# The second weight block of the FFN input matrix: its sum S2 made during the mixing stage, S1 and S3 made later

## The chip, the cores and the metric

The kernel runs on one core of a Trainium2 chip. The metric is the device time of one execution in microseconds (us). PE is the matrix engine (TensorE), DVE the vector engine (VectorE), ACT the scalar engine (ScalarE), POOL is GpSimd, and SP the engine that only issues transfers here. Every engine works off its own queue of instructions in order.

## The reference, cut to what matters

One layer of a streaming encoder, one sequence of 1024 rows with 1024 channels, all in float32. A mixing sub-layer ends with an output projection, `x = x + g1 * (merged @ w_o)`. The feed-forward sub-layer (FFN) follows:

```
h2 = rms_norm(x, norm_ffn_g) * (1 + sc2) + sh2
a, bgate = split(h2 @ w_ffn_in)              # w_ffn_in: 1024 x 5632
x = x + g2 * ((silu(a) * bgate) @ w_ffn_out) # then a last rms_norm
```

The change concerns the product `h2 @ w_ffn_in`, and the stage with `w_o` before it.

## The kernel before, in words

**Arithmetic on PE.** A float32 operand is split into a high and a low part. `split_w` (L214) does it for a weight tile of 128 x 1024: ACT writes the high part `wh` with a cast (L220), DVE the low part `wl` with a subtraction (L221). There are three buffers for `wh` and three for `wl`, so the split of a product's weights has to wait until the product three places before is done. Each block of a product then takes three matmuls (`mm3`, L340): `wh` with the high activations (L348), `wh` with the low ones (L349), `wl` with the high ones (L351). One product is 24 matmuls of 128 x 512.

**Seven products instead of eight.** A "dual" is a weight block of two by two tiles 11, 12, 21, 22, which is multiplied with two by two blocks of activations by a Strassen-Winograd scheme in seven products, run in the order `PRODUCTS = "1265734"`. Products 1, 2 and 4 use the tiles 11, 12 and 22 as they are. The others use sums of tiles: product 5 uses S1 = 21 + 22, product 7 uses S3 = 21 + 11, product 6 uses S2 = 11 + S1, and product 3 uses 12 + S2. `dual_units` (L227) returns for each product a function that loads what is missing, adds and splits. The adds run on DVE: S1 at L240, S3 at L242, S2 at L244, 12 + S2 at L261. With `early == 2` product 6 loads 21, 22 and 11 and makes all three sums, each in place (S1 in the buffer of 22, S3 in that of 21, S2 in that of 11), and products 5 and 7 only split.

**Loads.** `load` (L204) takes the next buffer of 4 KB per partition for a raw tile and issues the transfer on SP. The buffers rotate over two pools (`rawp` with three, `rawbp` with two); a third pool, `raw_a` with one, joins at the start of the FFN (L1231). SP waits for the buffer that a transfer needs, with all later transfers behind it. `next_w` and `fetch` make the units of a list `plan` two products ahead.

**Order of the stages here.** `mix(i, h)` (L1020) makes one block of the projection with `w_o`, for the half `h` of the rows: 24 matmuls, a DVE instruction that adds the residual (L1028), a transfer out, a square on ACT (L1030) and a running sum on DVE (L1036). With `h == 1` and `i == 0` it is followed by `norm_2_first` (L1053): all of the normalised activations of the first half of the rows. The last five `w_o` tiles of the second half are split again while this runs. Then the FFN starts. The first products are ordered by `in_order` (L1104), as (dual, product): (0,1) (0,2) (1,1) (1,2) (2,1), then 6 5 7 3 4 of dual 0, then 6 5 7 3 4 of dual 1, then dual 2 and so on, eleven duals. Between them DVE and ACT make the activations that the products need: `norm_2_half` (L1062; the tiles x, t2 with their parts t2h and t2l) and `norm_2_sums` (L1073; t5, t7, t3, t4 with high and low parts, split at L388 and L389, and the subtractions for t4 at L393).

**Orders written out by hand.** `tc.issue_after(ins)` queues an instruction behind another one of its engine. `in_unit` (L1107) queues the adds and splits of (0,7), (0,3), (0,4) and (1,6) behind the splits of the activations traced before. `in_evac` (L1134) reads the results out of the accumulators: for dual 0 it queues the add of product 3 (L1150) behind `dual_units.ins`, the last S2 that was traced, and what follows behind the split traced last. All else is ordered by a scheduler, by the order in which the program text gives the instructions and by when they could run.

**Memory.** The pool `diff` has one buffer of 1054 elements per partition, used by the depthwise convolution (`conv`, L823), long before. It and the pool `uc` are closed at the fifth product after the first five (L1230), and what is opened then lies over them: by the allocation, the buffer of `raw_a` and the second of the two `x1a` buffers overlap that of `diff`.

Of the kernel before, what the change touches and what calls it, by code (L numbers as in the profile page):

```python
# [35 lines left out]
F32 = mybir.dt.float32  # L36
F32R = mybir.dt.float32r
AF = mybir.ActivationFunctionType
ALU = mybir.AluOpType

P = 128
D = 1024
T = 1024
# [3 lines left out]
FC = DFF // P  # L47
SK = 3
CK = 31
# [32 lines left out]


AHEAD = 2

# [19 lines left out]
PRODUCTS = "1265734"  # L107
# [14 lines left out]
def block_kernel(ctx: ExitStack, tc: tile.TileContext, x0, xT, c, vecs, ada, w_first, w_plain, w_duals,  # L122
                 w_short, w_conf, w_o, w_fi, w_fo, w_last, outT):
    nc = tc.nc
# [4 lines left out]
    def open_pool(name, bufs, stack=None, **kw):  # L129

        p = tc.tile_pool(name=name, bufs=bufs, reuse_waits="tile", **kw)
        return p, (stack.enter_context(p) if stack else p.__enter__())
# [16 lines left out]
    ucp, diffp = (p for _, p in phase_1)  # L149
# [17 lines left out]
    def f32(t):  # L167
        return t.bitcast(F32)
# [28 lines left out]
    raws = [rawp] * 3 + [rawbp] * 2  # L197

    def raw_tile(n=1024):

        raws.append(raws.pop(0))
        return raws[-1].tile([P, 1024], F32, tag="raw", name="raw")[:, :n]

    def load(src, n=1024):  # L204
        raw = raw_tile(n)
        nc.sync.dma_start(raw, src)
        return raw

    pool_los = []
# [4 lines left out]
    def split_w(raw, n, after=(), lo_engine=nc.vector):  # L214
        wh = whp.tile([P, 1024], F32R, tag="wh", name="wh")[:, :n]
        wl = wlp.tile([P, 1024], F32R, tag="wl", name="wl")[:, :n]
        with ExitStack() as order:
            for ins in after:
                order.enter_context(tc.issue_after(ins))
            hi = nc.scalar.copy(wh, raw)  # L220
            lo = lo_engine.tensor_tensor(wl, raw, f32(wh), ALU.subtract)  # L221
        split_w.hi, split_w.lo = hi.ins, lo.ins
        if n == T and lo_engine is nc.gpsimd:
            pool_los.append((hi.ins, lo.ins))
        return wh, wl

    def dual_units(mats, n, early=0, eng=nc.vector):  # L227


        a = {}  # L230

        def get(*blocks):
            for b in blocks:
                a[b] = load(mats[("11", "12", "21", "22").index(b)], n)

        def sums(which):

            if "1" in which:
                a["s1"] = a["22"] if early == 2 else raw_tile(n)
                eng.tensor_tensor(a["s1"], a["21"], a["22"], ALU.add)  # L240
            if "3" in which:
                eng.tensor_tensor(a["21"], a["21"], a["11"], ALU.add)  # L242
            if "2" in which:
                dual_units.ins = eng.tensor_tensor(a["11"], a["11"], a["s1"], ALU.add).ins  # L244

        def unit(m):
            if early == 2:
                get(*{"1": ("11",), "2": ("12",), "6": ("21", "22", "11"), "3": ("12",), "4": ("22",)}.get(m, ()))
            elif early:
                get(*{"1": ("11",), "2": ("12", "21", "22", "11")}.get(m, ()))  # L250
            elif m == "1":
                get("11", "12", "21", "22")
            if m in "12":
                w = split_w(a["1" + m], n, (), eng)
                if eng is nc.gpsimd:
                    sums("13" if m == "1" else "2")
                return w
            if m == "6" and eng is not nc.gpsimd:
                sums("132")
            if m == "3":  # L260
                eng.tensor_tensor(a["12"], a["12"], a["11"], ALU.add)  # L261
            return split_w(a[{"6": "11", "5": "s1", "7": "21", "3": "12", "4": "22"}[m]], n, (), eng)

        return {m: (lambda m=m: unit(m)) for m in PRODUCTS}

    def apart_units(mats, eng):

# [40 lines left out]

    def next_w(ahead=AHEAD):

        fetch(ahead + 1)
        return ready.pop(0)
# [71 lines left out]
    def t_pair(name):  # L384
        return hl_tile(name + "h"), hl_tile(name + "l")

    def t_split(src, hi, lo):
        t_split.act = nc.scalar.copy(hi, src).ins  # L388
        t_split.ins = nc.vector.tensor_tensor(lo, src, f32(hi), ALU.subtract).ins  # L389
# [12 lines left out]
    def rstd_end(ss, eps, r, t, exp):  # L402

        nc.vector.scalar_tensor_tensor(out=t, in0=r, scalar=-0.5, in1=r, op0=ALU.mult, op1=ALU.mult)
        nc.vector.scalar_tensor_tensor(out=t, in0=ss, scalar=eps, in1=t, op0=ALU.add, op1=ALU.mult)
        nc.vector.scalar_tensor_tensor(out=r, in0=t, scalar=1.5, in1=r, op0=ALU.add, op1=ALU.mult)
        return r
# [38 lines left out]
    def first_w(k):  # L446

        w = next_w(min(AHEAD, KC - 1 - k))
        if k >= KC - KEPT:
# [48 lines left out]
    def norm_start(acc, name, n=H, tile_of=g_tile, ss_tile=ps_tile):  # L498
        ss = ss_tile("ss")
        acc = acc if isinstance(acc, list) else [acc]  # L500
        for t in acc:
            norm_start.ins = nc.tensor.matmul(ss[:, :n], ones, t, start=t is acc[0], stop=t is acc[-1]).ins
        return rstd_start(ss, eps1, name, n, tile_of)
# [106 lines left out]
    def again_w(i):  # L610

        if i < KEPT:
            fetch(i // 2)
            return kept.pop(0)
        return next_w(1 if i < KC - 2 else AHEAD)

# [305 lines left out]
    def load_b(i):  # L922

        loaded.append((i, load(ada[i])))
        if len(loaded) > 1:
            with tc.issue_after(split.ins):
                modulation_of(*loaded.pop(0))
# [110 lines left out]
    def h2_of(k, h, r2, hi_lo=None):  # L1038

        t = x1[k][:, halves[h]]  # L1040
        nc.vector.scalar_tensor_tensor(out=t, in0=t, scalar=aff2[:, k : k + 1], in1=r2, op0=ALU.mult, op1=ALU.mult)
        if hi_lo:
            hi, lo = hi_lo
            nc.scalar.activation(hi, t, AF.Identity, bias=modc(24 + k))
            nc.vector.scalar_tensor_tensor(
                out=lo, in0=t, scalar=modc(24 + k), in1=f32(hi), op0=ALU.add, op1=ALU.subtract
            )
        nc.scalar.activation(t, t, AF.Identity, bias=modc(24 + k))
        return t
# [3 lines left out]
    def norm_2_first():  # L1053

        r2 = rstd_end(*norm_start(sums[0], "r2"))
        for k in range(KC):
            ts["12"[k // KH]][k % KH] = hl = t_pair(f"h2{k}")
            h2_of(k, 0, r2, hl)
# [14 lines left out]
    def norm_2_sums(m):  # L1073
# [3 lines left out]
        with tc.issue_after(t_split.ins), tc.issue_after(t_split.act):  # L1077
# [5 lines left out]
            for k in range(KH):  # L1083
                ts[m][k] = t_pair("t" + m)
                t_split({"5": x1[k][:, halves[0]], "7": b12[k], "3": b22[k], "4": b21[k]}[m], *ts[m][k])

    sums = {}
    for h in range(2):
        for i in range(KC):
            mix(i, h)  # L1090
            if h == 0:
                load_b(32 + i)
            if (h, i) == (0, KC - 1):
                modulation_of(*loaded.pop())
            if h == 1 and i == 0:
                for k in range(KC):
                    affine(aff2, k, 32, vec, V_GFFN)
                norm_2_first()


    N_IN = FC // 2
    EARLY = [2, 2, 1] + [0] * (N_IN - 3)
    in_units = [dual_units([w_fi[d, m] for m in range(4)], 1024, EARLY[d]) for d in range(N_IN)]
    in_order = [(0, "1"), (0, "2"), (1, "1"), (1, "2"), (2, "1")] + [(d, m) for d in range(2) for m in PRODUCTS[2:]]  # L1104
    in_order += [(d, m) for d in range(2, N_IN) for m in PRODUCTS if (d, m) != (2, "1")]

# [7 lines left out]
    ha = {}  # L1114
    in_banks = [{} for _ in range(N_IN)]

# [84 lines left out]
    def group_load(g, m):  # L1201
        to[g, m] = [t_load((g * GROUP + i, m)) for i in range(GROUP)]

    def in_product(d, m, between=None):
        late = EARLY[d] == 1
        if late and m == "2":
            for p in range(2):
                in_evac(d)(p, "1", in_banks[d]["x", p])
        product(in_banks[d], m, ts[m], None if late and m == "1" else in_evac(d), between,
                z_tile=ps2_tile if d in (0, 2) else ps_tile)  # L1210
        if d == N_IN - 1:
            group_load(0, m)
# [13 lines left out]
    for i, (d, m) in enumerate(in_order[5:]):  # L1226
        if i < 4:
            norm_2_sums("5734"[i])
        elif i == 4:
            close(*phase_1)  # L1230
            raws.append(open_pool("raw_a", 1, side="right", stack=ctx)[1])  # L1231
            x1ap = open_pool("x1a", 2, side="right", stack=ctx)[1]
            phase_2 = [open_pool("gi", 7), open_pool("stage", 3, side="right")]
            gip, stagep = (p for _, p in phase_2)
        with ExitStack() as order:
            if d < 2:
                order.enter_context(tc.issue_after(mm3.ins))
            in_product(d, m)
        if m == PRODUCTS[-1]:
            if 2 <= d < 6:  # L1240
                with tc.issue_after(in_evac.ins):
                    for b in range(40 + 2 * (d - 2), 42 + 2 * (d - 2)):
                        modulation(b, x1ap.tile([P, T], F32, tag="x1", name="ada"))
            hid_set(d)
# [24 lines left out]
    n = 2 * GROUP * P  # L1269
# [20 lines left out]
    for f in range(REST, FC, 2):  # L1290
        for oh in range(2):
            raw = load(w_last[(f - REST) // 2, oh])
# [161 lines left out]
```

## Time and profile before

| | |
|---|---|
| median of three runs | 1476.24 us (1476.24 to 1478.43) |
| the profiled execution, its own time | 1477.93 us |
| its span, first to last instruction | 1476.2 us |
| PE busy | 1462.0 us, 99% |
| DVE busy | 1177.7 us, 80% |
| ACT busy | 617.0 us, 42% |
| POOL busy | 513.3 us, 35% |
| moved by transfers | 245.36 MB, mean 166 GB/s |

All times within the run are us from the start of the span. A row of a timeline gives start, duration, engine, line, operation and tiles, and in brackets how long the engine had been idle before and what released it; a duration of a matmul reaches over the start of the next one, so the distance of two starts is what a matmul costs. A row by stages gives for each engine its busy time and the number of instructions, then the clock granted to PE and the share of the transfer engines.

### The profile page before, as it was taken

Reading aid. Unit: us, or ns where it says so; the run is one execution under the profiler, and the core shown is the slowest. Engines: PE = TensorE matmul, PEld = TensorE weight load, DVE = VectorE, ACT = ScalarE, POOL = GpSimd, SP = SyncE. Lnnn points to the kernel's source line nnn. Section 1 sums busy time; section 2 is a strip of 40 time slices with the busy share of each in tenths; the row PEclk is TensorE's granted clock in tenths of the full one; section 3 lists DMA queues with packets and bytes.
Section 4 is the critical chain, followed back from the end, with each engine's and each line's share of the span. In section 5 each row is a group of like instructions: output and inputs, shape, how many; then the busy total and the mean of one; then the engine's idle time right before and its main releaser. Section 6 shows DMA issues by size and latency. Waiting matters only on the chain.

```text
span 1476.2 us, 17809 instructions
## 1 busy us (share of the span) xinstructions
PE 1462.0 (99%) x6475; PEld 1200.4 (81%) x6475; DVE 1177.7 (80%) x1623; ACT 617.0 (42%) x896; POOL 513.3 (35%) x459
## 2 busy tenths in 40 slices
PE   9999999999999999999999999999999999999997
PEld 5888888888888888878888878888888888888887
DVE  7999888887998969999687699777777765677755
ACT  4653433333333335555235465444444443222235
POOL 0036677767877771111022001101111015535005
PEclk9999999999999999999999999999999999999999
DMA  8522213222222267376685337655455449988403
GB/s 342 188 64 72 100 58 128 72 86 100 91 67 86 82 219 285 105 237 213 200 311 172 117 100 235 209 176 168 150 192 166 146 149 371 357 287 276 156 1 115
DMA packets 83274, 245.36 MB, mean 166 GB/s; under 512 B 9585, under 2 KB 11761, under 8 KB 83186
## 3 DMA queue, kind: packets, MB, share of 16 engines
q1 hardware_dynamic: 42352, 136.01, 27.6%
q0 software_dynamic: 36944, 95.44, 19.6%
q10 hardware_dynamic: 3890, 12.78, 2.3%
q8 instruction: 51, 0.84, 0.2%
q14 instruction: 37, 0.30, 0.1%
HBM read 181.79 MB, written 62.39 MB: 165 GB/s over the span
## 4 chain that ended last, share of the span: by engine, by line
PE 91%; DVE 6%; DMA 1%; issue 1%; ACT 1%; POOL 0%; POOLq 0%; DVEq 0%; ACTq 0%
PE bank L351 11%; PE bank L348 11%; PE bank L349 11%; PE x L351 7%; PE x L348 7%; PE x L349 7%; PE z L349 4%; PE z L348 4%; PE z L351 4%; PE y L349 3%; PE y L348 3%; PE y L351 3%; PE yb L351 2%; PE yb L348 2%; PE yb L349 2%; PE mix L349 2%
## 5 line engine op out<-in xcount | busy, mean ns | idle before, releaser
L220 ACT CAST wh<-raw 128x1024 fp32r<-128x1024 f32 (+2 forms) x254 | 256.3, 1011 | 485.2 <-PE bank L349 133.6
L221 POOL TENSOR_TENSOR wl<-raw,wh 128x1024 fp32r<-128x1024 f32 x84 | 204.5, 2444 | 81.8 <-ACT wh L220 81.8
L221 DVE TENSOR_TENSOR wl<-raw,wh 128x1024 fp32r<-128x1024 f32 (+2 forms) x170 | 195.0, 1147 | 47.5 <-ACT wh L220 46.2
L838 DVE SCALAR_TENSOR_TENSOR c<-diff,vec,c 128x512 f32<-128x512 f32 x232 | 171.0, 753 | 4.4
L1170 POOL DMA_DIRECT2D hid<-stage x71 | 37.8, 533 | 347.0 <-DVE stage L389 341.0
L348 PE MATMUL bank<-th,wh 128*128 128x512 f32 x288 | 112.0, 389 | 0.0
L349 PE MATMUL bank<-tl,wh 128*128 128x512 f32 x288 | 112.0, 389 | 0.0
L351 PE MATMUL bank<-th,wl 128*128 128x512 f32 x288 | 112.0, 389 | 0.0
L838 DVE SCALAR_TENSOR_TENSOR c<-u,wsum,c 128x512 f32<-128x512 f32 x112 | 84.3, 753 | 2.6
L240 POOL TENSOR_TENSOR raw<-raw 128x1024 f32<-128x1024 f32 x12 | 29.2, 2430 | 130.4 <-DVE wl L221 92.8
L388 ACT CAST stage<-g 128x512 fp32r<-128x512 f32 x62 | 38.4, 622 | 65.9 <-DMA hid<-stage 35.4
L351 PEld LDWEIGHTS bank<-th,wl 128*128 128x128 f32 x288 | 54.1, 188 | 11.3
L349 PEld LDWEIGHTS bank<-tl,wh 128*128 128x128 f32 x288 | 54.1, 188 | 11.2
L348 PEld LDWEIGHTS bank<-th,wh 128*128 128x128 f32 x288 | 54.1, 188 | 11.2
L389 DVE TENSOR_TENSOR stage<-g,stage 128x512 fp32r<-128x512 f32 x62 | 42.4, 689 | 25.3 <-ACT stage L388 25.3
L1196 POOL DMA_DIRECT2D th<-hid x71 | 38.0, 535 | 53.2 <-PE x L351 31.9
L348 PE MATMUL x<-th,wh 128*128 128x512 f32 x144 | 56.1, 390 | 0.0
L349 PE MATMUL x<-tl,wh 128*128 128x512 f32 x144 | 56.0, 389 | 0.0
L351 PE MATMUL x<-th,wl 128*128 128x512 f32 x144 | 56.0, 389 | 0.0
L348 PE MATMUL yb<-zsh,wh 128*128 128x512 f32 x128 | 49.8, 389 | 0.0
L349 PE MATMUL yb<-zsl,wh 128*128 128x512 f32 x128 | 49.8, 389 | 0.0
L351 PE MATMUL yb<-zsh,wl 128*128 128x512 f32 x128 | 49.8, 389 | 0.0
(798 smaller groups left out, 4211.3 us busy)
## 6 DMA issues: line engine op xcount, KB each, us to landing
hid<-stage POOLq DMA_DIRECT2D x71, 512.0 KB, 4.4
raw<-in_w_fi SPq DMA_DIRECT2D x51, 512.0 KB, 3.7
raw<-in_w_duals SPq DMA_DIRECT2D x48, 512.0 KB, 3.5
th<-hid POOLq DMA_DIRECT2D x71, 256.0 KB, 5.7
tl<-hid POOLq DMA_DIRECT2D x71, 256.0 KB, 5.7
ada<-in_ada SPq DMA_DIRECT2D x24, 512.0 KB, 5.9
raw<-in_ada SPq DMA_DIRECT2D x24, 512.0 KB, 4.6
raw<-in_w_fo SPq DMA_DIRECT2D x24, 384.0 KB, 5.7
```

Of the source, the lines that this page charges most:

```text
L220: hi = nc.scalar.copy(wh, raw)
L221: lo = lo_engine.tensor_tensor(wl, raw, f32(wh), ALU.subtract)
L240: eng.tensor_tensor(a["s1"], a["21"], a["22"], ALU.add)
L348: nc.tensor.matmul(ps, wh, xh, start=first, stop=False, skip_group_check=again)
L349: nc.tensor.matmul(ps, wh, xl, start=False, stop=False, skip_group_check=again)
L351: mm3.ins = nc.tensor.matmul(ps, wl, xh, start=False, stop=last, skip_group_check=again).ins
L388: t_split.act = nc.scalar.copy(hi, src).ins
L389: t_split.ins = nc.vector.tensor_tensor(lo, src, f32(hi), ALU.subtract).ins
L838: tap.ins = nc.vector.scalar_tensor_tensor(out=out, in0=src[:, s : s + H], scalar=wt, in1=acc, op0=ALU.mult, op1=ALU.add).ins
L1170: nc.gpsimd.dma_start(hid_dram[key], s)
L1196: nc.gpsimd.dma_start(t, hid_dram[key][:, s])
```

## The change

For dual 1 alone, the generator `begin` makes S2 ahead of time, in three steps behind the blocks 2, 3 and 4 of the second half of `mix` (`S2_AT`). Step one loads 21 and 22. Step two adds S1 in the buffer of 22 and loads 11. Step three adds S2 = 11 + S1 into the buffer of `diff`. Each load is queued behind the last load traced before it. Product 6 of dual 1 then only splits S2; product 5 loads 21 and 22 once more and makes S1, product 7 loads 11 once more and makes S3, product 3 adds S2 to 12 as before. `raw_a` is still opened at the same place, but joins the rotation four products later. The rest of the diff moves the making of `in_units` ahead of the `mix` loop.

```diff
+S2_AT = (2, 3, 4)
...
     def load(src, n=1024):
         raw = raw_tile(n)
-        nc.sync.dma_start(raw, src)
+        load.ins = nc.sync.dma_start(raw, src).ins
         return raw
...
+        def begin():
+            with tc.issue_after(load.ins):
+                get("21", "22")
+            yield
+            eng.tensor_tensor(a["22"], a["21"], a["22"], ALU.add)
+            with tc.issue_after(load.ins):
+                get("11")
+            yield
+            a["s2"] = diffp.tile([P, T + CK - 1], F32, tag="diff", name="s2")[:, :n]
+            eng.tensor_tensor(a["s2"], a["11"], a["22"], ALU.add)
+            yield
+
+        def unit_begun(m):
+            get(*{"1": ("11",), "2": ("12",), "5": ("21", "22"), "7": ("11",), "3": ("12",), "4": ("22",)}.get(m, ()))
+            if m == "5":
+                sums("1")
+            elif m == "7":
+                sums("3")
+            elif m == "3":
+                eng.tensor_tensor(a["12"], a["12"], a["s2"], ALU.add)
+            return split_w(a[{"1": "11", "2": "12", "6": "s2", "5": "s1", "7": "21", "3": "12", "4": "22"}[m]], n, (), eng)
+
         def unit(m):
+            if "s2" in a:
+                return unit_begun(m)
...
+            if h == 1 and i in S2_AT:
+                next(in_units[1]["begin"])
...
-            raws.append(open_pool("raw_a", 1, side="right", stack=ctx)[1])
+            raw_a = open_pool("raw_a", 1, side="right", stack=ctx)[1]
...
+        elif i == 8:
+            raws.append(raw_a)
```

More of the change, by code (lines that the diff above doesn't have):

```diff
@@ L262, in unit @@
             return split_w(a[{"6": "11", "5": "s1", "7": "21", "3": "12", "4": "22"}[m]], n, (), eng)
-        return {m: (lambda m=m: unit(m)) for m in PRODUCTS}
+        return {m: (lambda m=m: unit(m)) for m in PRODUCTS} | {"begin": begin()}
     def apart_units(mats, eng):
@@ L1085, in norm_2_sums @@
                 t_split({"5": x1[k][:, halves[0]], "7": b12[k], "3": b22[k], "4": b21[k]}[m], *ts[m][k])
+    N_IN = FC // 2
+    EARLY = [2, 2, 1] + [0] * (N_IN - 3)
+    in_units = [dual_units([w_fi[d, m] for m in range(4)], 1024, EARLY[d]) for d in range(N_IN)]
     sums = {}
@@ L1098, in block_kernel @@
                 norm_2_first()
-    N_IN = FC // 2
-    EARLY = [2, 2, 1] + [0] * (N_IN - 3)
-    in_units = [dual_units([w_fi[d, m] for m in range(4)], 1024, EARLY[d]) for d in range(N_IN)]
+            if h == 1 and i in S2_AT:
+                next(in_units[1]["begin"])
     in_order = [(0, "1"), (0, "2"), (1, "1"), (1, "2"), (2, "1")] + [(d, m) for d in range(2) for m in PRODUCTS[2:]]
```

## The prediction

> **What bounds the kernel now.** I read the page first, then the waits of PE, then the timelines of PE, DVE and ACT around the place that they name.
>
> ```profile
> PE 1462.0 (99%) x6475; PEld 1200.4 (81%) x6475; DVE 1177.7 (80%) x1623; ACT 617.0 (42%) x896; POOL 513.3 (35%) x459
> PE 91%; DVE 6%; DMA 1%; issue 1%; ACT 1%; POOL 0%; POOLq 0%; DVEq 0%; ACTq 0%
> ```
>
> PE is busy for 1462.0 of 1476.2 us, so the number of matmuls sets the time, and this change alters none of them. An edit can only win where PE stands still. The second line is the chain that ended last: 6% of it lies on DVE, so somewhere DVE sets the pace.
>
> ```profile
> PE lead L344 <- ACT x L432: 2.3, 1, 2.3
> PE x L348 <- ACT wh L220: 1.2, 1, 1.2
> PE clock L535 <- DVE eps L183: 1.1, 1, 1.1
> PE bank L348 <- ACT wh L220: 0.6, 2, 0.4
> ```
>
> These are all of PE's listed waits (total, times, longest). The first and third are in the opening, the fourth in the products with the short convolution. The second, 1.2 us for a cast of weights, is in the FFN. The timeline of PE shows it:
>
> ```profile
> 876.16 0.62 PE L348 MATMUL x<-t4h,wh 128*128 128x512 f32 x2
> ...
> 881.37 0.39 PE L351 MATMUL x<-t4h,wl 128*128 128x512 f32 x1
> 882.98 0.50 PE L348 MATMUL x<-t2h,wh 128*128 128x512 f32 x1 [1.22 <-ACT wh L220]
> ...
> 888.92 0.39 PE L348 MATMUL z<-t5h,wh 128*128 128x512 f32 x1
> ...
> 894.36 0.39 PE L348 MATMUL x<-t7h,wh 128*128 128x512 f32 x1
> ```
>
> t4 is product (0,4), t2 here product (1,6), then come (1,5) and (1,7). From 888.92 to 894.36 one undisturbed product takes 5.44 us, 0.227 for each of 24 matmuls. The last matmul of (0,4) starts at 881.37, so (1,6) could start at 881.60 and (1,5) 5.44 later, at 887.04. It starts at 888.92. The stall at the head of (1,6), with the waits for `wl` in its first matmuls, costs 888.92 - 887.04 = 1.9 us. What DVE and ACT do meanwhile:
>
> ```profile
> 875.62 2.50 DVE L389 TENSOR_TENSOR t4l<-x,t4h 128x512 fp32r<-128x512 f32 x4
> 878.03 1.22 DVE L240 TENSOR_TENSOR raw<-raw 128x1024 f32<-128x1024 f32 x1
> 879.29 1.23 DVE L242 TENSOR_TENSOR raw<-raw 128x1024 f32<-128x1024 f32 x1
> 880.55 1.22 DVE L244 TENSOR_TENSOR raw<-raw 128x1024 f32<-128x1024 f32 x1
> 881.69 1.28 DVE L1150 TENSOR_TENSOR g<-z,g 128x512 f32<-128x512 f32 x2
> 882.96 1.22 DVE L221 TENSOR_TENSOR wl<-raw,wh 128x1024 fp32r<-128x1024 f32 x1
> ```
> ```profile
> 873.94 2.43 ACT L388 CAST t4h<-x 128x512 fp32r<-128x512 f32 x4
> 881.88 2.00 ACT L220 CAST wh<-raw 128x1024 fp32r<-128x1024 f32 x2 [5.52 <-DVE raw L244]
> ```
>
> DVE works without a pause: the low parts of t4, then S1, S3 and S2 of dual 1, and only after S2 can ACT cast the weights of (1,6). ACT has been idle for 5.52 us before that cast. So the stall is the three adds, 1.2 us each, in front of the cast.
>
> ```profile
> 786.00:826.00 40.00, 40.00 (x176) 32.75 (x175) 29.73 (x39) 22.29 (x32) 7.57 (x14) 1.00 0.58 184
> 826.00:859.00 33.00, 32.87 (x143) 26.22 (x142) 28.95 (x40) 18.12 (x29) 0.54 (x1) 1.00 0.24 72
> 859.00:882.00 23.00, 22.76 (x101) 18.52 (x99) 22.78 (x32) 14.57 (x24) 0.00 (x0) 1.00 0.44 137
> 882.00:900.00 18.00, 16.96 (x73) 13.73 (x74) 16.31 (x22) 11.62 (x18) 3.72 (x7) 1.00 0.68 221
> 900.00:1200.00 300.00, 300.00 (x1325) 248.40 (x1324) 222.16 (x278) 132.43 (x194) 31.91 (x60) 1.00 0.54 176
> ```
>
> By stages (after the length: busy PE, weight load, DVE, ACT, POOL; then PE clock): DVE fills 22.78 of the 23 us ahead of the stall, but 29.73 of 40 in the second half of mix, where the adds go. From 900 to 1200 PE does not pause. The second row lacks 0.13 us of PE, which I leave in place.
>
> **The change, part by part.** *Product 6 of dual 1.* Its three loads and three adds go from this place. ACT has cast t4h by 873.94 + 2.43 = 876.4, the cast of S2 (2.00 / 2 = 1.0 us) follows to 877.4, and DVE comes to its `wl` at 878.03 and is done at 879.3. (1,6) can start at 881.60: the whole 1.9 us goes, cover 2.3 us. S2 is long ready by then if the part in mix holds.
>
> *S1 at product 5, S3 at product 7.* Both adds stay on DVE, one and two products later. What is next late is (1,5), wanted by PE at 887.04. After 879.3 DVE has the reads of product 3 at L1150 (1.28 the pair), their multiplications (one pair more of that size), S1 (1.2), then the cast (1.0) and `wl` (1.2): 879.3 + 1.28 + 1.28 + 1.2 + 1.0 + 1.2 = 885.3. Should the pair that reads product 4 fall in between too, 886.5. Cover 0.5 to 1.7 us, so nothing on the path. S3 for (1,7) has 5.44 us more of PE time for 1.2 + 1.0 + 1.2 = 3.4 us of work. The adds that remain here are two of three, so DVE is 1.2 us lighter in the stage.
>
> ```profile
> 854.91 18.15 SPq L206 DMA_DIRECT2D raw<-in_w_fi  x5
> ```
> ```profile
> raw<-in_w_fi SPq DMA_DIRECT2D x18, 512.0 KB, 3.6
> ```
>
> *Their loads.* These five transfers of before are 21, 22, 11, 12 and 22 of dual 1, issued when the raw buffers of dual 0 come free, the last by 854.91 + 18.15 = 873.06, and landed 3.6 us later (median of 18 issues), 876.7. The new program asks for the same five in the same order, on the same buffers' release, ahead of an S1 that DVE reaches after 881. Cost nothing; the cover is some 5 us.
>
> *What is added in mix.* Three loads of 512 KB on SP and two adds of 1.2 us on DVE, in the order of the text behind blocks 2, 3 and 4 (S1 is made twice in all, so DVE does five adds for this dual where it did four).
>
> ```profile
> 766.96 6.48 SPq L206 DMA_DIRECT2D raw<-in_w_o  x4
> 789.00 84.06 SPq L206 DMA_DIRECT2D raw<-in_w_fi  x15
> ```
> ```profile
> 786.90 0.75 DVE L1028 SCALAR_TENSOR_TENSOR x<-mix,mod,xr 128x512 f32<-128x512 f32 x1 [3.25 <-PE mix L351]
> 787.75 1.23 DVE L221 TENSOR_TENSOR wl<-raw,wh 128x1024 fp32r<-128x1024 f32 x1
> ...
> 800.49 1.22 DVE L221 TENSOR_TENSOR wl<-raw,wh 128x1024 fp32r<-128x1024 f32 x1
> ...
> 815.00 0.75 DVE L1028 SCALAR_TENSOR_TENSOR x<-mix,mod,xr 128x512 f32<-128x512 f32 x1 [2.76 <-PE mix L351]
> ```
> ```profile
> 803.92 0.39 PE L348 MATMUL mix<-mg01h,wh 128*128 128x512 f32 x1
> ...
> 825.68 0.39 PE L348 MATMUL x<-h20h,wh 128*128 128x512 f32 x1
> ```
>
> SP has issued the last `w_o` tiles by 773.44 and stands until 789.00. The loads of 21 and 22 take two of those places, so they land before 780, while DVE has a hole of 3.25 us before 786.90. From 786.90 on it works through `norm_2_first` and the splits; before 815.00 there is a hole again, of 2.76 us. Two adds fit in such holes: 0 us, the value I take. If both fall between the two holes, they push the split at 800.49 by 2.4 us. It ends at 801.71; its block starts on PE at 803.92 and needs `wl` at its third matmul, 0.45 later, a cover of 2.7 us. So 0 there too; only beyond 2.7 us does PE wait (a rival below). Below nothing is excluded, since PE has no gap in mix to give back. The three loads hold three raw buffers, so `w_o` tiles and the first FFN tiles wait for others. The first FFN tile, issued at 789.00 now, is needed on PE at 825.68; with 3.6 us of load and 2.2 of cast and split it may come some 30 us later. Cost nothing.
>
> *S2 kept until product 3; `raw_a` later.* One raw buffer fewer until then. Duals from the third on have 38 us each (7 products of 5.44) for loads of 3.6, so from 0 to the 1.2 us of one add that comes late; I take 0, by the row 900 to 1200 without a PE pause.
>
> **Sum.** -1.9 us + 0. The profiled execution (1477.93, span 1476.2 and 1.7 around it) would become 1476.0. It lies 1.69 above the median of 1476.24, which becomes 1474.3, 0.13% less. About 0.2%, 3 us, is what a measurement of this kernel can tell from no change: the forecast stays within it.
>
> **Rivals.** *1. The order at product 4 turns against it.* (1,6) is queued behind the splits of t4, but S1 and the split of (1,5) are not, nor is L1150 any longer behind dual 1's sums. t4l starts at 875.62 and PE wants t4 from 876.16: hardly any cover. If S1 and a `wl` slip in ahead of it, 2.4 us, PE stands some 2 us at (0,4) instead: 1474.3 + 2.0 = 1476.3, no change. For: the scheduler fills holes. Against: DVE shows none there to fill. A part of it, 0.6 us for one L1150, gives 1474.9.
>
> *2. Slower: DVE held in mix.* DVE takes its queue in order. If the two adds are queued behind 787.75 and stand there for their loads, all of `norm_2_first` and the splits of `w_o` stand behind them. For two waits in a row: 3.6 + 1.2 + 0.5 (issue of the second load) + 3.6 + 1.2 = 10.1 us, less 2.7 of cover, 7.4 us of PE stall, net +5.5: 1481.7. It decides from 2.7 us of held DVE on, and ends above the 3 us when more than 1.9 + 3.0 + 2.7 = 7.6 us are lost. One load with its add (4.8 us) gives 2.1, net +0.2. Against: loads and adds are a block of 5.44 us apart, more than 3.6. The granted clock stays 1.00 in the row with the stall (882 to 900). The Trainium skill's page "TensorE: Matmul & The Clock Gate", Part 1, says that the PE clock falls to half after an idle window of about 3.4 us and needs about as long of work to come back. By it the 1.9 us that go take no slow matmuls with them, which agrees with that 1.00, and a stall of 7.4 us would cost some 1.7 us more (an estimate from that page: half of 3.4), 1483.4; no run here shows such a stall in mid-run.
>
> *3. More than 0.2% faster.* The profile has no place for it beyond 1.9 + 0.13; only the spread of the runs (2.2 us) could show it.
>
> **Chances.** Forecast 0.58; rival 1 0.15, within the 0.2%; rival 2 and its like (a raw buffer short by so much) 0.20; rival 3 0.07. So faster 0.07, same 0.73, slower 0.20. The range goes from 1472.6 (forecast with most of the spread) to 1479.8 (a new PE stall of 5.5 us, between rival 2's one load and its two).
>
> **What would show it.** Right: PE runs (0,4) into (1,6) into (1,5) at 0.227 us; the three adds are gone between t4l and the `wl` of (1,6); two adds stand in holes of DVE in mix, up to 820; ACT's 5.52 us idle before the cast is gone. Wrong: a PE wait at (0,4) or (1,5) for t4l or `wl` (rival 1), or one in mix with DVE waiting on raw<-in_w_fi before 800 (rival 2).

## The result, and the profile after

| | before | after |
|---|---|---|
| median | 1476.96 us (6 runs, 1476.24 to 1480.24) | 1482.68 us (6 runs, 1480.48 to 1484.87) |
| span of the profiled execution | 1476.2 us | 1481.1 us |

The change makes the kernel slower by 0.3%: ratio 1.0032, with a 95% interval of 1.0019 to 1.0044. The forecast was 1474.3 us with a range up to 1479.8; the result lies above it. From here on times are those of one profiled execution each, and line numbers are those of the changed kernel (about 30 higher than before in the FFN: the reads of y are L1171, before L1141; the reads of product 3 L1180, before L1150).

The busy times of the page, the shares of its chain, and four of PE's waits in the changed kernel (total, times, longest):

```profile
PE 1463.3 (99%) x6475; PEld 1200.5 (81%) x6475; DVE 1178.0 (80%) x1624; ACT 615.7 (42%) x896; POOL 514.0 (35%) x459
...
PE 69%; issue 21%; DVE 4%; POOL 3%; DMA 2%; ACT 1%; POOLq 0%; DVEq 0%; ACTq 0%
```
```profile
PE z L376 <- DVE g L1171: 2.8, 1, 2.8
...
PE x L376 <- DVE g L1175: 0.8, 2, 0.6
PE x L377 <- DVE t4l L417: 0.7, 1, 0.7
...
PE ss L530 <- DVE xr L1064: 0.4, 1, 0.4
```

The work is the same; the waits are not. The 1.2 us for `wh` is gone and others have come. (`ss` is the matmul over the running sum of squares, one for each half of the rows; the wait listed is at the second, whose place lost 0.3 us before and 0.5 now.) The timeline of PE, at the heads of (0,4), (1,6), (1,5) and (2,5):

```profile
875.16 0.61 PE L376 MATMUL x<-t4h,wh 128*128 128x512 f32 x2
876.48 0.50 PE L377 MATMUL x<-t4l,wh 128*128 128x512 f32 x1 [0.70 <-DVE t4l L417]
...
881.64 0.39 PE L376 MATMUL x<-t2h,wh 128*128 128x512 f32 x1
...
887.08 0.39 PE L376 MATMUL z<-t5h,wh 128*128 128x512 f32 x1
...
919.80 0.39 PE L379 MATMUL x<-t2h,wl 128*128 128x512 f32 x1
923.00 0.75 PE L376 MATMUL z<-t5h,wh 128*128 128x512 f32 x1 [2.81 <-DVE g L1171]
923.55 0.63 PE L377 MATMUL z<-t5l,wh 128*128 128x512 f32 x1
923.98 0.63 PE L379 MATMUL z<-t5h,wl 128*128 128x512 f32 x1
924.40 0.63 PE L376 MATMUL z<-t5h,wh 128*128 128x512 f32 x1
```

(1,6) takes 887.08 - 881.64 = 5.44 us: the old stall has gone as forecast, 1.9 us. At (0,4) PE waits about 1.0 us for `t4l`. At (2,5) two starts lie 3.20 us apart instead of 0.23, a loss of 3.0, and the matmuls behind it start 0.43 apart instead of 0.227 until 926.5: the product takes 7.17 us (923.00 to 930.17) instead of 5.44, another 1.7. Smaller waits at 906, 979, 1007 and 1056 add 2.2. Gains and losses make +6.0 us; from the head of (0,4) to the end of the span the changed kernel takes 1481.1 - 875.16 = 605.9 us and the old one 1476.2 - 876.16 = 600.0.

Why (2,5) waits: its accumulators z take the two banks in which the results y of (2,2) still stand, until DVE has read them. The timelines of PE and DVE before, then of DVE after:

```profile
921.56 0.39 PE L348 MATMUL z<-t5h,wh 128*128 128x512 f32 x1
...
919.65 1.28 DVE L1141 TENSOR_TENSOR g<-y,g 128x512 f32<-128x512 f32 x2
```
```profile
899.80 0.69 DVE L1175 TENSOR_TENSOR g<-x,g 128x512 f32<-128x512 f32 x1
903.21 0.69 DVE L417 TENSOR_TENSOR stage<-g,stage 128x512 fp32r<-128x512 f32 x1 [2.72 <-ACT stage L416]
903.82 1.22 DVE L243 TENSOR_TENSOR raw<-raw 128x1024 f32<-128x1024 f32 x1
...
922.17 1.28 DVE L1171 TENSOR_TENSOR g<-y,g 128x512 f32<-128x512 f32 x2
```

Before, the first of the two reads (0.69 us each) is done at 920.34 and (2,5) starts at 921.56: 1.2 us to spare. After, the first read is done at 922.86 and (2,5) starts 0.14 later; so PE could have come 1.1 us earlier before, and no more. (Two of the expectations below count 0.6 us, to the end of the second read.) On the way DVE has stood 2.72 us for a cast of ACT into a stage buffer. The waits of DVE from 882 to 925, before and after, the same stretch by stages (length; busy PE, weight load, DVE, ACT, POOL; PE clock, share and GB/s of the transfer engines), and ACT's cast:

```profile
DVE stage L389 <- ACT stage L388: 3.2, 5, 0.9
```
```profile
DVE stage L417 <- ACT stage L416: 6.2, 4, 2.7
```
```profile
882.00:925.00 43.00, 41.96 (x184) 34.42 (x185) 39.48 (x52) 24.74 (x39) 7.91 (x15) 1.00 0.65 219
```
```profile
882.00:925.00 43.00, 40.18 (x173) 32.62 (x172) 35.28 (x47) 20.04 (x32) 7.46 (x14) 0.98 0.67 233
```
```profile
902.55 0.62 ACT L416 CAST stage<-g 128x512 fp32r<-128x512 f32 x1 [3.93 <-DMA hid<-stage]
```

DVE works 4.2 us less in the same 43 us (39.48 to 35.28), mostly because ACT waits for one of the three stage buffers to be stored, 3.93 us at this cast. The stores land late. The issues of SP before and after, and the landing times of the transfers of `hid` issued from 885 to 909 (view of that tensor, before and after):

```profile
876.94 0.80 SPq L324 DMA_DIRECT2D ada<-in_ada  x2
```
```profile
889.73 1.97 SPq L352 DMA_DIRECT2D ada<-in_ada  x2
```
```profile
DMA to landing us min/median/max: 3.3/4.7/6.6
```
```profile
DMA to landing us min/median/max: 3.7/7.4/10.2
```

The second of the two x1a buffers lies over S2, so the pair of ada transfers (2 x 512 KB) now waits until 12 + S2, begun at 888.10, is made and goes behind the first two of the seven stores, ahead of the others; before, it went at 876.94 and had landed, 4.7 us at most, well before the first store was issued (889.76). The Trainium skill's page "DMA: Bandwidth & Descriptors", section on queues, rings and completion order, says that each transfer engine goes round between the queues that have work; by that, two transfers of SP's queue stretch those of POOL's beside them, which agrees with 4.7 becoming 7.4 us (of the seven stores alone, 5.0 becoming 6.7).

Ahead of all this, DVE's order at t4 (timeline after):

```profile
864.52 1.22 DVE L243 TENSOR_TENSOR raw<-raw 128x1024 f32<-128x1024 f32 x1
...
875.74 0.69 DVE L417 TENSOR_TENSOR t4l<-x,t4h 128x512 fp32r<-128x512 f32 x1
876.34 0.69 DVE L1180 TENSOR_TENSOR g<-z,g 128x512 f32<-128x512 f32 x1
876.94 0.69 DVE L417 TENSOR_TENSOR t4l<-x,t4h 128x512 fp32r<-128x512 f32 x1
877.54 0.69 DVE L1180 TENSOR_TENSOR g<-z,g 128x512 f32<-128x512 f32 x1
878.14 0.69 DVE L417 TENSOR_TENSOR t4l<-x,t4h 128x512 fp32r<-128x512 f32 x1
878.74 1.22 DVE L245 TENSOR_TENSOR raw<-raw 128x1024 f32<-128x1024 f32 x1
879.87 0.69 DVE L417 TENSOR_TENSOR t4l<-x,t4h 128x512 fp32r<-128x512 f32 x1
```

S1 of dual 1 (L243) is made between the splits of t7, and S3 (L245) and the reads of product 3 between those of t4. All of them used to stand behind t4l. The handle `dual_units.ins` that held the reads back now belongs to dual 0, since dual 1 no longer passes the line that sets it. S1 and S3 used to be made with the weights of (1,6), which `in_unit` queues behind the splits of t4; now they belong to (1,5) and (1,7), which it does not. The 1.0 us at `t4l` is S1's: PE reaches (0,4) 1.0 us earlier than before, DVE was 1.0 us earlier too (L1108 at 860.90, as L1080 before at 861.93), and S1 uses that up with its 1.1 us in the queue, so that t4l starts at 875.74 where it started at 875.62.

### The profile page after: what moved, and what is told of

It is laid out like the page before. It is cut to its first block, busy times and chain, and to the rows that moved or that the text cites. A ratio compares the mean times of both kernels' runs of the same rounds, so it can differ in the third digit from the quotient of the medians.

```text
span 1481.1 us, 17821 instructions
## 1 busy us (share of the span) xinstructions
PE 1463.3 (99%) x6475; PEld 1200.5 (81%) x6475; DVE 1178.0 (80%) x1624; ACT 615.7 (42%) x896; POOL 514.0 (35%) x459
## 4 chain that ended last, share of the span: by engine, by line
PE 69%; issue 21%; DVE 4%; POOL 3%; DMA 2%; ACT 1%; POOLq 0%; DVEq 0%; ACTq 0%
PE bank L379 11%; PE bank L377 11%; PE bank L376 11%; PE x L376 5%; PE x L377 5%; PE x L379 5%; PE z L376 2%; PE z L377 2%; PE z L379 2%; PE y L376 2%; PE y L379 2%; PE y L377 2%; DMA hid<-stage 2%; PE lead L379 1%; PE lead L376 1%
## 5 line engine op out<-in xcount | busy, mean ns | idle before, releaser
L243 POOL TENSOR_TENSOR raw<-raw 128x1024 f32<-128x1024 f32 x12 | 29.2, 2432 | 130.5 <-DVE wl L224 92.0
L243 DVE TENSOR_TENSOR raw<-raw 128x1024 f32<-128x1024 f32 (+1 forms) x17 | 19.2, 1130 | 46.8 <-DMA raw<-in_w_fi 42.5
```

## The experiments

Every ratio is to the kernel before on the same chip, with its 95% interval. The kernel before had medians of 1477.5 to 1478.4 us there.

**Does the lost load buffer cost it?** The kernel before, with `raw_a` joining four products later:

```diff
-            raws.append(open_pool("raw_a", 1, side="right", stack=ctx)[1])
+            raw_a = open_pool("raw_a", 1, side="right", stack=ctx)[1]
+        elif i == 8:
+            raws.append(raw_a)
```


> The kernel before with one part of the change alone: the buffer raw_a joins the rotation four products later. Rival 'rotation': 3 to 6 us above the kernel before, with PE waits in duals 2 to 5. Theory 'collision': 0 to 1.5 us above it, from the sum S1 of dual 2 that is made one instruction later.

1.0003 (0.9994 to 1.0013). This part costs nothing that can be measured by itself; the prediction's 0 for it holds.

**Does the late ada pair cost it?** First the kernel before with its first ada pair held back on SP behind a load of dual 2, to 887.8 and 890.7:

```diff
-                with tc.issue_after(in_evac.ins):
+                with ExitStack() as late:
+                    late.enter_context(tc.issue_after(in_evac.ins))
+                    if d == 2:
+                        late.enter_context(tc.issue_after(in_unit.second))
```


> The kernel before with one edit: its two first ada transfers are queued on SP behind the load of tile 21 of dual 2, so they start at about 889 us as in the changed kernel instead of at 876.9; the order on PE, DVE, ACT and POOL stays. Theory 'collision': median landing of hid<-stage between 885 and 908 us rises from 5.0 to over 6 us, DVE reads y of (2,2) about 2 us later, PE waits 1 to 2.5 us at (2,5) (its cover in the kernel before is 0.6 us), time 1 to 4 us above the kernel before. Rival 'rotation': within 0.5 us of the kernel before.

1.0012 (1.0003 to 1.0020), and a wait at (2,5) appears in the old kernel (waits of PE):

```profile
PE z L350 <- DVE g L1146: 1.0, 1, 1.0
```

So the late pair alone uses up the 1.2 us and costs one more. Its way there is only in part the expected one: the median landing of the stores rises from 5.0 to 5.4 us, not to over 6, while DVE's waits for stage casts (882 to 925) go from 3.2 to 5.4 us. Then the changed kernel with the pair held back to 914.1, behind the last load traced:

```diff
+                    if d == 2:
+                        late.enter_context(tc.issue_after(load.ins))
```


> The changed kernel with one edit: the first two ada transfers (512 KB each, for dual 2) are queued on SP behind a later weight load, so that they leave the stretch 889 to 902 us; the order on PE, DVE, ACT and POOL stays. Theory 'collision' (these transfers now wait for the buffer of S2, start at 889.7 instead of 876.9 and slow the hid<-stage stores, so that DVE reads y of product (2,2) late and PE waits at (2,5)): median landing of hid<-stage between 885 and 908 us back from 6.7 to about 5 us, the PE wait of 3.2 us at (2,5) down to 1.3 us or less, no matmuls at 0.427 us behind it, 4 to 5 us less than the changed kernel, about 1478. Rival 'rotation' (the raw buffer that joins four products later delays the sums of dual 2): the wait at (2,5) stays over 2.5 us, at most 1 us less than the changed kernel.

1.0022 (1.0012 to 1.0033). The waits behind 925 have gone, the matmuls behind (2,5) run at full rate and the median landing of the stores is back at 5.1 us, but the wait at (2,5) itself stays at 3.2 us, start to start. Waits of PE and of DVE (882 to 925):

```profile
PE z L376 <- ACT stage L416: 2.8, 1, 2.8
```
```profile
DVE stage L417 <- ACT stage L416: 5.9, 5, 1.7
```

(The view names ACT's cast; DVE's first read of y ends at 924.01, 0.14 us before PE starts, as in the changed kernel.) So half of the expectation fails, and the gain is about 1.5 us instead of 4 to 5. DVE still stands 5.9 us for stage casts, and one store still lands in 8.1 us. Raw loads are issued among the stores at 887.8, 890.8 and 896.3; but the kernel before has loads there too (888.9, 891.8, the next at 900.9), so it is not shown that they do it.

**Is it the address alone?** The convolution's buffer is given up ahead of S2, and `raw_a`, opened there, is S2's buffer, under no x1a:

```diff
-            a["s2"] = diffp.tile([P, T + CK - 1], F32, tag="diff", name="s2")[:, :n]
+            close(phase_1.pop())
+            raw_as.append(open_pool("raw_a", 1, side="right", stack=ctx)[1])
+            a["s2"] = raw_as[0].tile([P, 1024], F32, tag="raw", name="s2")[:, :n]
```


> The changed kernel with another address for S2: the convolution's buffer is given up ahead of S2, raw_a is opened there and then, and its one buffer is S2 until product 3, so the second x1a buffer no longer lies under S2 and the first pair of ada transfers need not wait for S2. Order of DVE, ACT and POOL as in the changed kernel. Theory 1 (the overlap is the whole loss): ada transfers start at about 877 as in before, hid transfers land in about 5 us, no wait at (2,5), no waits after 925, ratio 0.999 to 1.000. Theory 2 (the overlap is a part; one load buffer less and the order of DVE are the rest): ada and hid as in theory 1, the waits after 925 are gone, but PE waits 1.5 to 3.2 us at (2,5) and 0.9 us for t4l; ratio 1.001 to 1.0025.

1.0019 (1.0010 to 1.0029): theory 2. The profiled execution was the fastest of this kernel's eleven (1476.6; they reach 1483.8), so its small wait at (2,5), 0.3 us, says little on the median. Overlap or not, about 0.2% is left.

**Is it the banks?** The changed kernel with the accumulators z of dual 2 from the pool of six:

```diff
-                z_tile=ps2_tile if d in (0, 2) else ps_tile)
+                z_tile=ps2_tile if d == 0 else ps_tile)
```


> The changed kernel with one edit: the two accumulators of product (2,5) come from the pool of six instead of the pool of two in which y of (2,2) still waits to be read; the order on every engine is the same. If the late read of y alone holds PE at (2,5): the wait of 3.2 us there goes, and with it the 9 slow matmuls behind it (0.427 instead of 0.227 us, 1.8 us): 4.8 us less than the changed kernel, about 1478. If DVE as a whole is behind by then: PE waits at the next product for weights or reads instead, and at most 2 us are gained.

1.0024 (1.0013 to 1.0034). The wait at (2,5) goes and comes back at 938, 978 and 1008 (waits of PE):

```profile
PE x L376 <- DVE g L1175: 4.1, 2, 2.1
...
PE x L376 <- ACT g L1169: 1.5, 1, 1.5
```

The second possibility of the expectation holds, only further on. The bank is where PE meets DVE; it is DVE that is behind.

**The order at t4.** The changed kernel with both halves of an order written out:

```diff
-                with behind(d, dual_units.ins):
+                with behind(d, t_split.ins):
...
+        norm_2_sums.last = t_split.ins, t_split.act
...
+            for ins in norm_2_sums.last if d == 1 and m in "573" else ():
+                order.enter_context(tc.issue_after(ins))
```


> The changed kernel, with the two reads of product 3 of dual 0 and the adds and splits of (1,5), (1,7) and (1,3) queued behind the last split of t4. Both theories: the PE wait for t4l at 875 (0.9 us) goes. Theory A: 0.9 us faster than the changed kernel, ratio to before 1.0025 or so. Theory B: PE only comes to (2,5) 0.9 us earlier and waits there longer, 3.0 to 4 us, hid transfers still land in about 7 us, the ratio stays at 1.003.

1.0000 (0.9992 to 1.0009). Both theories fall: A forecast 1.0025, B 1.003, and the whole loss is gone, 4.7 us by the ratios, though the wait at t4l was 1.0 us. There is no wait at (2,5). From the head of (0,4) to the end of the span this run takes 598.1 us, 2.0 less than the kernel before, so in its profile the stall's gain is kept there; on the other side the first `ss`, in mix, starts 1.1 us late. DVE's waits from 882 to 925 and the same stretch:

```profile
DVE stage L417 <- ACT stage L416: 2.0, 3, 0.9
```
```profile
882.00:925.00 43.00, 43.00 (x192) 35.60 (x191) 39.20 (x51) 23.70 (x35) 7.57 (x15) 1.00 0.75 247
```

With the sums later, 12 + S2 comes at 895.57 instead of 888.10, the ada pair at 897.2 and 899.8, behind five of the seven stores, and DVE stands 2.0 us instead of 6.2. The two halves were run apart. Only the reads (the first line of the diff):

> The changed kernel with one half of the order at t4: only the two reads of product 3 of dual 0 are queued behind the last split of t4. The scheduler then puts S1 and also 12 + S2 of dual 1 among the four t4l, so S2 is free ten us sooner and the first ada pair can go at about 880, ahead of the hid stores. Theory P (what costs is where the ada pair and the late loads lie against the hid stores, by way of DVE's waits for stage casts): PE waits 1 to 2 us at t4l, DVE waits for stage casts about 3 us between 882 and 925 as in before, no wait over 1 us at (2,5); ratio 1.0000 to 1.0012. Theory Q (the wait at t4l sets all that follows late): as slow as the changed kernel or slower, ratio 1.003 or more.

Only the sums (the rest of it):

> The changed kernel with the other half of the order at t4: only the adds and splits of (1,5), (1,7) and (1,3) are queued behind the last split of t4; the reads of product 3 stay among the t4l. The scheduler now puts 12 + S2 behind the first five stage splits, so S2 is free later and the ada pair goes at about 897, behind most hid stores. Theory P: PE waits 0.3 to 0.6 us at t4l, DVE waits for stage casts 2 to 3 us, no wait over 1 us at (2,5); ratio 1.0000 to 1.0008, near that of the run with the whole order. Theory Q: the wait at t4l is halved and so is the loss, ratio 1.0015.

1.0006 (0.9997 to 1.0016) and 0.9991 (0.9982 to 1.0000): theory P's ranges hold for the first and are beaten by the second, theory Q (as slow as the change, or half of it) falls. (The expectation for the first says S1; the add among the t4l is S3, S1 stands further ahead.) So the direct wait at t4l is not the loss: with the reads alone PE still loses 1.7 us there. And it comes from the sums: with their order alone PE does not wait there, though the reads still stand among the t4l. What P says of the second run is only partly right: its pair went at 893.6 and 897.1, stores took up to 8.6 us and DVE stood 4.6 us for casts where it expected 2 to 3, but the scheduler's new order reads the first y at 915.24, several places sooner.

**The sum with fewer adds.** The kernel before, with the three adds of dual 1 cut to 8 columns, so that most of the sums is left out (one of the three is shown). The weights of (1,5), (1,7) and (1,3) are queued behind the last split of t4 as in the run with the sums alone, which keeps DVE's order as it was up to 902 us:

```diff
-                eng.tensor_tensor(a["s1"], a["21"], a["22"], ALU.add)
+                eng.tensor_tensor(a["s1"][:, :part], a["21"][:, :part], a["22"][:, :part], ALU.add)
```


> The kernel before; the three adds of dual 1 (S1, S3, S2 ahead of product (1,6)) are cut to 8 of their 1024 columns, so most of the sums is left out, and the adds in place stay where they were in DVE's queue. No transfer, no buffer and (up to (1,6)) no order changes. It is the gain of the change by itself: DVE 3.4 us shorter in front of the cast. Theory A (a matmul stall that goes is a gain wherever it is): the 1.9 us at (1,6) go, no new wait, 1.9 us faster, ratio 0.9987. Theory B (the read of y, due at (2,5) with 0.6 us to spare, hangs on casts, stores and loads that do not move with PE): the 1.9 us at (1,6) go and 0.5 to 1.5 us of it come back as a PE wait at the head of (2,5), near 920; ratio 0.9990 to 1.0000.

0.9988 (0.9979 to 0.9996): theory A, with no wait at (2,5). The stall's 1.9 us can be had, 1.8 measured, when DVE is 3.4 us lighter as well, for then the reads of y come sooner too (table below).

**Mending it.** The order at t4, S2 in `raw_a`, and S2's add in mix behind the running sum that the ss matmul waits for:

```diff
-        def begin():
+        def begin(behind_s2=lambda: mix.sums[0]):
...
+            with tc.issue_after(behind_s2()):
+                eng.tensor_tensor(a["s2"], a["11"], a["22"], ALU.add)
```


> The changed kernel with three edits together: S2 in raw_a (no overlap), the order at t4 (as in the run on that order), and S2's add in mix queued behind the running sum that the ss matmul waits for. Theory 1 (overlap and the two orders are the loss): none of the waits is left, 1.9 us faster than before, ratio 0.9987. Theory 2 (the chain of casts, stores and loads to the read of y sets (2,5) whatever PE does): no wait at ss and t4, no waits after 925, but 1 to 3 us at (2,5); ratio 0.9995 to 1.001.

0.9992 (0.9983 to 1.0001), between the two theories; there is no wait at (2,5), which is theory 1's sign. With z in the pool of six besides:

> The kernel with S2 in raw_a, the order at t4 and S2's add behind the running sum, and besides the accumulators z of dual 2 from the pool of six, so (2,5) need not wait for the reads of y. If (2,5) still costs something in some executions, this is faster than without it, ratio to before 0.9985; if DVE's lag only shows further on, as with z alone, it is the same or slower, 0.9990 to 1.0005, with PE waits after 930.

0.9993 (0.9983 to 1.0002): the same as without it. And with only the sums' half of the order:

> The run that queues only the adds and splits of (1,5), (1,7) and (1,3) behind the last split of t4 (ratio 0.9991), with the two other edits put to it: S2 in raw_a, so the first ada pair goes at about 876, and S2's add behind the running sum that ss waits for. Order of DVE otherwise the same. If the overlap still costs something when the order is right: the waits of that run near 972 and 1001 (3 us) and the one at ss (1 us) go, hid transfers land in 5 to 6 us, ratio 0.9975 to 0.9986, below that of before by more than its interval. If PE's pauses in dual 3 and later are paid by executions that differ anyway: the same ratio, 0.9989 to 0.9995.

0.9990 (0.9980 to 0.9999). In the three profiles PE loses no more than 0.7 us at any one place from 785 to 1200. The second possibility of the last expectation holds: beside 0.9991, the address and the add in mix bring nothing that can be measured once the order is right. The last run has the lowest ratio of the complete kernels, some 1.5 us below the kernel before, of which the interval leaves little sure; from 0.9991 to 0.9993 it can't be told apart.

**What orders the runs.** From the profiles: the time from the head of (0,4) to the end of DVE's first read of y for (2,5). PE needs eight products for that way, 8 x 5.44 = 43.5 us, and its own waits. The table was put together after the runs; none of them was made to test it.

| run | first y read done, us after (0,4) | ratio |
|---|---|---|
| only the sums' order, raw_a, mix (sums_mended) | 39.0 | 0.9990 |
| before, raw_a later (before_raw_late) | 40.3 | 1.0003 |
| only the sums' order (t4_sums) | 41.0 | 0.9991 |
| whole order, raw_a, mix (mended) | 41.9 | 0.9992 |
| whole order at t4 (t4_order) | 42.1 | 1.0000 |
| before, short adds (short_adds) | 42.8 | 0.9988 |
| only the reads' order (t4_reads) | 43.7 | 1.0006 |
| before | 44.2 | 1 |
| S2 in raw_a (s2_in_raw_a) | 44.9 | 1.0019 |
| before, ada pair late (before_ada_late) | 46.4 | 1.0012 |
| ada pair at 914 (ada_later) | 47.4 | 1.0022 |
| changed kernel | 47.7 | 1.0032 |

Up to the 44.2 us of the kernel before, no interval lies above 1; beyond it, all do. The order within each half is not exact (one execution each; the runs with other banks for z are left out).

## Why the prediction was wrong

- **The stall at (1,6): right.** It goes as worked out, by (1,6) from 881.64 to 887.08 and by ACT's missing idle time of 5.52 us.
- **Adds in mix at 0: right within 0.15 us here, not in every execution.** They stand at 775.04 and 779.66, ahead of the holes that were named, each after a wait for its load (2.23 and 2.80 us). In this execution the first `ss` starts 0.15 us late; in the other profiles with S2's add at this place it is from nothing (t4_reads, t4_sums) to 1.1 (ada_later, t4_order) and 1.65 us (z_in_ps). Rival 2 is seen only in this small form. (Its sum has 0.5 us for the issue of a load; one on SP takes 0.33 in the trace before, which changes nothing here.)
- **The order after t4: the step that failed first.** The working put S1 behind t4l and a read of product 3, at about 881, and found a cover of 0.5 to 1.7 us for (1,5). No order held S1, S3 and the reads there any more. The prediction saw this as rival 1, "S1 and the split of (1,5) are not, nor is L1150 any longer behind dual 1's sums", and priced the direct wait at 0.6 to 2.0; it measured 1.0. It gave that a chance of 0.15 and took it for no change. What it left out is what follows: sums made early free raw buffers early, and move loads and 12 + S2 against the stores. With the sums alone put back behind t4 the ratio is 0.9991 instead of 1.0032.
- **"S2 kept until product 3; `raw_a` later ... I take 0": half of it failed.** `raw_a` later is 0. S2 kept until product 3 is not: its address lies under the second x1a buffer, which stands in the description of the memory, and nobody waits for that buffer but the ada pair. It was never followed. In the old order of sums the late pair costs about 0.12% (1.0012 by itself); with the sums behind t4, leaving the overlap or mending it makes no difference that can be measured (0.9991 and 0.9990).
- **"By the row 900 to 1200 without a PE pause": a wrong reading.** A row with no pause says that nothing was late by even a tenth, not by how much things were early. The first y read was done 44.2 us after the head of (0,4), and PE without its stall needs 43.5. Had DVE gone on as before, the 1.9 us would have met a new wait of 0.8 at (2,5). The gain could be kept only if DVE came sooner, as in the run with short adds.
- **The clock.** Rival 2's sentence on the Trainium skill ("TensorE: Matmul & The Clock Gate", Part 1) expected half the clock after an idle window of about 3.4 us. It came after a gap of 3.2 us in the changed kernel and cost 1.7 us, the size that the prediction estimated there for such a fall.

What stays open: of the 4.7 us between the changed kernel and the run with the order, the collision and the place of the y reads in DVE's queue were not separated to the end. The runs with an order at t4 moved both, since the scheduler orders anew after such an edit.

## What to carry to other kernels

When a stall of the bound engine is removed, everything behind it is wanted sooner by that much: work out the spare time at the next few places where it depends on the others, as time from a common point, and take the smallest as the gain. Follow each buffer's address to the next tenant and ask what transfer now waits, and beside which transfers it will then run. If an order is held by "behind the last one traced of this kind", an edit that no longer passes that line lets it go without a word in the diff.

## What the runs showed of the hardware that was not expected

Two gaps of PE of the same length had different consequences. The gap before (2,5) is 3.20 us from start to start in the changed kernel and 3.21 in the run with the ada pair later; behind the first, matmuls start 0.43 us apart up to 926.5, behind the second 0.227. The stretch around it, by stages, in the one and in the other:

```profile
915.00:930.00 15.00, 12.19 (x47) 9.65 (x47) 12.10 (x17) 8.91 (x14) 3.73 (x7) 0.89 0.80 268
```
```profile
915.00:930.00 15.00, 12.18 (x54) 9.79 (x54) 12.00 (x17) 8.65 (x14) 3.73 (x7) 1.00 0.92 309
```

The clock was 0.89 in the first and 1.00 in the second. The Trainium skill's page "TensorE: Matmul & The Clock Gate", Part 1, says that the window of about 3.4 us runs free, so that it depends on where in it the work lies. That agrees with one of two equal gaps being followed by slow matmuls, though a gap shorter than the window should not have been.

A store of 512 KB, which lands in 4.8 us in the median of all 71 stores of `hid` in the changed kernel, took up to 10.2 us (the row of `hid` above) where transfers of SP's queue were under way beside it.
